# Gate scaling of expert rows on ScalarE, the conditioning row applied in the output stage, a fifth high-part buffer, and small VectorE operations issued earlier

## The chip, the cores and the metric

One core of a Trainium2 chip runs the whole program. The metric is the device time of one execution in microseconds (us). The core has TensorE (matmuls, PE in the profile; its weight loads are PEld), VectorE (DVE), ScalarE (ACT), GpSimd (POOL), SyncE (SP, which here only issues DMAs) and 16 DMA engines.

## The reference

One layer of a decoder trunk on 512 tokens of width 1024, all in float32: a mixing sub-layer (retention and dilated attention), then a mixture of experts, then a final RMSNorm. The change touches the end of it:

```
mod = silu(c) @ w_ada + b_ada -> sh_a, sc_a, gt_a, sh_f, sc_f, gt_f     # rows of 1024
x = x + gt_a * (merged @ w_o)                                          # "x1"
h = rms_norm(x, g_ffn) * (1 + sc_f) + sh_f
top 4 of 32 experts per token, gates = softmax(top logits)
expert e: u = h @ w1[e] + b1[e]            # 1024 -> 2048
          a = min(u_even, 7) * sigmoid(1.702 * min(u_even, 7)) * (clip(u_odd, -7, 7) + 1)
          y_e = a @ w2[e] + b2[e]          # 1024 -> 1024
x = x + gt_f * sum over chosen e of gate[token, e] * y_e
out = rms_norm(x, g_final)
```

The conditioning row `gt_f` has one value per column and is the same for all tokens; the gate has one value per token and expert.

## The kernel before, in words

A float32 product is made on TensorE from parts: the high part of a weight tile is a rounded copy (ScalarE, line 1039, `prep_hi`), the low part is the tile less its high part (VectorE, line 1045, `prep_lo`), and TensorE multiplies high by high, high by low and low by high.

The first 700 us or so are the conditioning rows, attention, retention and the merge. Weight tiles there go through a pool `wr` of five buffers. Around line 678 a tile `z` of that pool is filled with zeros and written to the spare rows of two arrays in HBM, `acc` (line 682) and `xn2` (line 683). Before the experts, the stream x1 is written to the first 512 rows of `acc` (line 903, `x1_store`).

Then the experts run one after the other, the first two in fixed order, the others sorted by their number of tokens. Each works on a block of gathered token rows: 96 slots for a large expert (`KIND` "L"), 64 for a small one ("S"). The order is four large ones, then large and small in turn. An expert has 12 weight tiles of 1 MB: eight of `w1` ("A", k = 0 to 7, 8 KB rows) and four of `w2` ("B", k = 0 to 3, 4 KB rows). The list `tiles` holds the order A of expert e, then B of expert e−1, then A of e+1, and so on. The order on every engine in this stage is the order of the program text (`manual_schedule`): the loop over `tiles` issues the matmuls of tile i, then `prep_hi(i + 3)`, `prep_lo(i + 3)`, then the small operations that belong to this place.

The tiles are loaded by SyncE into a ring of ten buffers (five of `wr`, one of `wb`, four of `hl`); `prep_lo(i)` issues the load of tile i + 10 behind it, since it is the last reader of its buffer. The high parts have four buffers (tag `mg`), the low parts four (tag `lo`); each comes free when TensorE has done its tile. For a large expert a tile takes 12 matmuls; for a small one the high and low parts of its 64 rows lie side by side as 128, a tile takes 8 matmuls, and the two halves are added at the end by a copy on ScalarE (`lower`) and matmuls with a shifted identity (`fold`).

Small operations around it: `evacuate` (at B k=0) reads `u` out of PSUM into `sg` (sigmoid, ScalarE, line 1197) and `av` (VectorE, lines 1202 and 1206). `times_gate` (VectorE, line 1209) finishes `av`; it stands behind A k=1 of the next expert, and for the last one at B k=2. TensorE transposes `av` before its tiles A k=3 and k=4 (line 1175, `turn`), and ScalarE and VectorE copy it out in two parts (lines 1116 and 1117). `slot_hot` (line 1140, at A k=5) prepares the gather of a later expert. `close` calls `finish`: VectorE makes `ys` = `y` × gate × `gtF` (line 1215; `gtF` is `gt_f` repeated over the partitions, loaded at line 1131), and GpSimd adds the rows of `ys` to `acc` in HBM by a scatter DMA with addition (line 1216).

After a loop for experts with more tokens than slots, which runs as often as a list says, the output stage loads `acc` in four blocks of 128 rows, by halves of 512 columns (line 1480), sums squares on ScalarE (line 1483), and VectorE multiplies by the root and by `g_final` (line 1491), and SyncE stores.

Of the kernel before, what the change touches and what calls it, by code (L numbers as in the profile page):

```python
# [11 lines left out]
F32 = mybir.dt.float32  # L12
F32R = mybir.dt.float32r
# [8 lines left out]
P = 128  # L22
# [14 lines left out]
NRA = 5  # L37
NRB = 1
NRC = 4
AHEAD = 3  # L40
TB = 1536
ROWS = S + P
# [71 lines left out]
def body(tc, a, out):  # L114
# [11 lines left out]
    def bcast(ap, off, n, parts=P):  # L126
        return dram(ap, off, [[0, parts], [1, n]])
# [9 lines left out]
    xn2 = nc.dram_tensor("s_h2", [ROWS, D], F32).ap()  # L137
    acc = nc.dram_tensor("s_acc", [ROWS, D], F32).ap()
    modr = nc.dram_tensor("s_mod", [1, 4096], F32).ap()
    btab = nc.dram_tensor("s_bias", [4, 896], F32).ap()  # L140
# [540 lines left out]
    G.memset(z, 0.0)  # L681
    G.dma_start(acc[S:], z)
    G.dma_start(xn2[S:], z)
# [105 lines left out]
    mx = ExitStack()  # L789
    wb = mx.enter_context(tc.tile_pool(name="wrB", bufs=NRB, side="right", reuse_waits="tile"))  # L790
    rt = mx.enter_context(tc.tile_pool(name="rt", bufs=1, side="right", reuse_waits="tile"))
# [90 lines left out]

    ring = [(wr, "wr")] * NRA + [(wb, "wb")] * NRB + [(hl, "hl")] * NRC
    rs = {}
# [7 lines left out]
    def half_row(t, n):  # L892
        return xs[:, t, n * 512:(n + 1) * 512]
# [8 lines left out]
    def x1_store(t, n):  # L902
        SP.dma_start(acc[t * P:(t + 1) * P, n * 512:(n + 1) * 512], half_row(t, n))

# [112 lines left out]
    sorted_i = rt.tile([1, E], I32, name="sorted_i")  # L1017
    for i in range(NRA + NRB):
        load(i, *ring[i])
# [14 lines left out]
    for k in range(NRC):  # L1034
        load(NRA + NRB + k, *ring[NRA + NRB + k])
    def prep_hi(i):
        if i < len(tiles) and i not in his:
            his[i] = mp.tile([P, 2048], F32R, name="w_hi", tag="mg")
            A.activation(his[i], loaded[i], AF.Copy)  # L1039
# [80 lines left out]
    for q in range(2):  # L1120
        turn_copy(xp0[q], slice(4 * q, 4 * q + 4), X[0])
    for i in range(1, AHEAD):
        prep_hi(i) if i not in his else None
        prep_lo(i)
    psx.close()
# [3 lines left out]
    A.activation(top7[:, 1:2], top7[:, 0:1], AF.Sigmoid, scale=1.702)  # L1129
    gtF = m1.tile([P, D], F32, name="gtF")  # L1130
    G.dma_start(gtF, bcast(modr, 3 * D, D))

# [79 lines left out]
    def finish(y, gate, idx):  # L1212
        n = idx.shape[0]
        ys = m2.tile([CAP, D], F32, name="ys", bufs=1)[:n]
        V.scalar_tensor_tensor(ys, y[:n].rearrange("p a b -> p (a b)"), gate, gtF[:n], op0=OP.mult, op1=OP.mult)  # L1215
        G.indirect_dma_start(out=acc, out_offset=bass.IndirectOffsetOnAxis(ap=idx[:, :1], axis=0), in_=ys,  # L1216
                             in_offset=None, compute_op=OP.add)
# [79 lines left out]
    hot_at = {(0, 0): 1, (0, 2): 0}  # L1297
    hot_at.update({(e, 5): e + 2 for e in range(E - 2)})
    sum_at = {(0, 1): 1, (0, 4): 0}
# [15 lines left out]
    for i, (kind, e, k) in enumerate(tiles):  # L1315
# [33 lines left out]
        else:  # L1349
# [26 lines left out]
            if e == 0 and k == 0:  # L1376
                ld = overflow_list()
        prep_hi(i + AHEAD)
        prep_lo(i + AHEAD)
        if kind == "A":  # L1380
            if nx is not None:
                SL[nx] = slot_rows(now["ps"], nx > 0)
            if e == 0 and k == 0:
                sort_counts()
            if (e, k) in hot_at:
                h_ = hot_at[e, k]
                now["oh"] = slot_hot((rk1 if h_ < 2 else rkp)[:, :, h_], slots_of(h_))
            if e and k == 1:
                AVS[e - 1] = times_gate(SG.pop(e - 1), AVS[e - 1])
            if e > 1 and k == 0:  # L1390
                close(e - 2)
            if e and k in (3, 4):
                if k == 3:
                    AT[e - 1] = at_tiles(e - 1)
                turn_copy(now["at", k - 3], slice(4 * (k - 3), 4 * (k - 3) + 4), AT[e - 1])
            if e + 1 < E and k in (5, 6):
                if k == 5:
                    X[e + 1] = x_tiles(e + 1)
                turn_copy(now["xt", k - 5], slice(4 * (k - 5), 4 * (k - 5) + 4), X[e + 1])
            if k == KC - 1:  # L1400
                if KIND[e] == "S":
                    now["low"] = lower(U[e])
                if e == 0:
                    evacuate(0)
            if e == 3 and k == 2:
                G.dma_start(lb.rearrange("p a b -> p (a b)"), bcast(ld, 0, 4 * E))
            if e == 5 and k == 2:
                V.tensor_copy(li, lb[0:1])
        else:
            if e + 1 < E:  # L1410
                if k == 0:
                    evacuate(e + 1)
                if e + 1 == E - 1 and k == 2:
                    AVS[e + 1] = times_gate(SG.pop(e + 1), AVS[e + 1])
                    AT[e + 1] = at_tiles(e + 1)
            if k == 3:
                if KIND[e] == "S":
                    now["ylow"] = lower(Y[e])
                if e >= E - 2:
                    close(e)  # L1420
# [3 lines left out]

    gfin = wr.tile([P, D], F32, name="gfin", tag="wr")
    SP.dma_start(gfin, bcast(a["g_final"], 0, D))
    extra = nc.values_load(li[0:1, 0, 2:3], min_val=0, max_val=E)  # L1427
    with tc.For_i(0, extra) as it:  # L1428
# [21 lines left out]
        for k in range(KC):  # L1450
            w = wb.tile([P, 2048], F32, name="w_x1", tag="wb")
            SP.dma_start(w, w1[0, ds(ev, 1)].rearrange("o (k p) n -> p (o k) n", p=P)[:, k])
            for j in range(4):
                PE.matmul(u[:, j], xT[:, k], w[:, j * 512:(j + 1) * 512], start=False, stop=(k == KC - 1))
# [9 lines left out]
        for k in range(4):  # L1464
            w = wb.tile([P, 2, D], F32, name="w_x2", tag="wb")
            SP.dma_start(w, w2[0, ds(ev, 1)].rearrange("o (k p) n -> p (o k) n", p=P)[:, 2 * k:2 * k + 2])
            for c in range(2):
                for n in range(2):
                    PE.matmul(y[:, n], aT[:, 2 * k + c], w[:, c, n * 512:(n + 1) * 512], start=False,
                              stop=(k == 3 and c == 1))  # L1470
# [3 lines left out]
    halves = [slice(n * 512, (n + 1) * 512) for n in range(2)]  # L1474
    at = [wr.tile([P, 2, D], F32, name="at", tag="wr") for _ in range(NT)]
    ss = [m2.tile([P, 2], F32, name="ss2", bufs=NT) for _ in range(NT)]
    with tc.manual_schedule():
        for t in range(NT):
            for c in halves:
                SP.dma_start(at[t][:, 0, c], acc[t * P:(t + 1) * P, c])  # L1480
        def scale_of(t):
            for n, c in enumerate(halves):
                A.activation(at[t][:, 1, c], at[t][:, 0, c], AF.Square, accum_out=ss[t][:, n:n + 1])  # L1483
            V.tensor_add(ss[t][:, 0:1], ss[t][:, 0:1], ss[t][:, 1:2])  # L1484
            return rms_cols(ss[t][:, 0:1], D, EPS, m2)
# [34 lines left out]
```

## Time and profile before

| | us |
|---|---|
| median of 3 runs (lowest, highest) | 1909.26 (1907.37, 1910.88) |
| profiled execution | 1909.79 |
| its span | 1908.0 |
| TensorE busy in the span | 1754.7 |
| VectorE busy | 1491.2 |
| ScalarE busy | 1052.6 |
| GpSimd busy | 463.7 |

The span runs from the first to the last instruction of the profiled execution; the execution's own time has 1.8 us around it. A busy TensorE is one that has a matmul in its pipeline. The granted clock is the share of TensorE's full speed (2.4 GHz) in a stretch. In a row of the waits, "A <- B" says that A's engine was idle until B was done. In a timeline a row ends with the idle time before it and what ended it.

### The profile page before, as it was taken

Reading aid. Unit: us, or ns where it says so; the run is one execution under the profiler, and the core shown is the slowest. Engines: PE = TensorE matmul, PEld = TensorE weight load, DVE = VectorE, ACT = ScalarE, POOL = GpSimd, SP = SyncE. Lnnn points to the kernel's source line nnn. Section 1 sums busy time; section 2 is a strip of 40 time slices with the busy share of each in tenths; the row PEclk is TensorE's granted clock in tenths of the full one; section 3 lists DMA queues with packets and bytes.
Section 4 is the critical chain, followed back from the end, with each engine's and each line's share of the span. In section 5 each row is a group of like instructions: output and inputs, shape, how many; then the busy total and the mean of one; then the engine's idle time right before and its main releaser. Section 6 shows DMA issues by size and latency. Waiting matters only on the chain. (4 is left out here: it accounts for less than half of the span.)

```text
span 1908.0 us, 23014 instructions
## 1 busy us (share of the span) xinstructions
PE 1754.7 (92%) x8369; PEld 1332.6 (70%) x8369; DVE 1491.2 (78%) x1506; ACT 1052.6 (55%) x968; POOL 463.7 (24%) x406
## 2 busy tenths in 40 slices
PE   5979999999999988999989989989889889889883
PEld 3868888888778865666666666666666667667662
DVE  7464535667653477999999999999999999999994
ACT  5133323222222334677677677677677677677672
POOL 2140001011110033253331231234462232232201
PEclk8999999999999989999999999999999999999997
DMA  9613333442673847999999999999999999999973
GB/s 313 167 45 97 103 90 117 123 117 84 180 184 111 297 149 269 326 382 361 367 381 348 369 380 355 373 378 358 372 373 371 368 381 361 368 379 359 373 298 103
DMA packets 206756, 521.27 MB, mean 273 GB/s; under 512 B 11974, under 2 KB 127094, under 8 KB 173744
## 3 DMA queue, kind: packets, MB, share of 16 engines
q1 hardware_dynamic: 197024, 492.36, 71.4%
q0 software_dynamic: 9616, 27.40, 6.1%
q8 instruction: 67, 1.10, 0.2%
q14 instruction: 49, 0.40, 0.1%
HBM read 501.57 MB, written 18.15 MB: 272 GB/s over the span
## 5 line engine op out<-in xcount | busy, mean ns | idle before, releaser
L1045 DVE TENSOR_TENSOR w_lo<-w_moe,w_hi 128x2048 fp32r<-128x2048 f32 x384 | 867.4, 2284 | 85.1 <-ACT w_hi L1039 84.5
L1039 ACT ACTIVATE w_hi<-w_moe 128x2048 fp32r<-128x2048 f32 x384 | 727.9, 1913 | 227.4 <-PE u L1339 164.3
L1339 PE MATMUL u<-w_hi,x 128*96 128x512 f32 x1152 | 315.8, 401 | 0.0
L1339 PEld LDWEIGHTS u<-w_hi,x 128*96 128x96 f32 x1152 | 180.3, 163 | 72.1 <-issue 0.2
L1216 POOL DMA_INDIRECT s_acc<-ys,idx x32 | 109.5, 3420 | 378.9 <-DVE ys L1215 368.5
L1155 POOL TENSOR_SCALAR sl<-sl,misc 96x1 f32<-96x1 f32 (+1 forms) x32 | 61.3, 1914 | 414.8 <-ACT sl L1154 414.8
L211 PE MATMUL pp<-hTh,w_hl 128*128 128x512 f32 x400 | 160.3, 401 | 0.0
L1339 PE MATMUL u<-w_lo,x 128*96 128x512 f32 x576 | 156.9, 394 | 0.0
L213 PE MATMUL pp<-hTh,w_hl 128*128 128x512 f32 x400 | 156.6, 391 | 0.0
L212 PE MATMUL pp<-hTl,w_hl 128*128 128x512 f32 x400 | 156.4, 391 | 0.0
L1364 PE MATMUL y<-w_hi,at 128*96 128x512 f32 x576 | 151.3, 396 | 0.0
L202 DVE TENSOR_TENSOR w_hl<-w_raw,w_hl 128x1024 fp32r<-128x1024 f32 (+1 forms) x66 | 87.8, 1343 | 76.4 <-ACT w_hl L201 76.4
L1344 PE MATMUL u<-w_hi,x 128*128 128x512 f32 x448 | 141.1, 440 | 0.0
L1344 PE MATMUL u<-w_lo,x 128*128 128x512 f32 x448 | 130.6, 417 | 0.0
L1364 PEld LDWEIGHTS y<-w_hi,at 128*96 128x96 f32 x576 | 91.7, 161 | 44.4 <-issue 5.9
L1339 PEld LDWEIGHTS u<-w_lo,x 128*96 128x96 f32 x576 | 93.5, 162 | 40.5
L1344 PEld LDWEIGHTS u<-w_lo,x 128*128 128x128 f32 x448 | 91.5, 204 | 22.5
L201 ACT ACTIVATE w_hl<-w_raw 128x1024 fp32r<-128x1024 f32 (+1 forms) x66 | 65.2, 1001 | 70.7 <-PE pp L213 54.0
L1175 PE MATMUL pt<-misc,av 96*128 96x96 f32 (+1 forms) x256 | 37.0, 274 | 70.9 <-DVE av L1209 70.9
L1344 PEld LDWEIGHTS u<-w_hi,x 128*128 128x128 f32 x448 | 85.8, 207 | 19.6 <-issue 5.4
L1175 PEld LDWEIGHTS pt<-misc,av 96*128 96x128 f32 (+1 forms) x256 | 28.6, 163 | 94.0 <-DVE av L1209 82.9
L211 PEld LDWEIGHTS pp<-hTh,w_hl 128*128 128x128 f32 x400 | 75.5, 189 | 18.0 <-issue 2.6
(344 smaller groups left out, 2922.9 us busy)
## 6 DMA issues: line engine op xcount, KB each, us to landing
w_moe<-in_w_mlp SPq DMA_DIRECT2D x384, 1024.0 KB, 7.9
w_raw<-in_w_in SPq DMA_DIRECT2D x76, 512.0 KB, 5.3
w_ada<-in_w_ada SPq DMA_DIRECT2D x24, 1024.0 KB, 5.4
w_raw<-in_w_ret_o SPq DMA_DIRECT2D x8, 512.0 KB, 4.3
w_o<-in_w_o SPq DMA_DIRECT2D x4, 1024.0 KB, 5.0
xin<-in_x SPq DMA_DIRECT2D x4, 512.0 KB, 6.6
w_raw<-in_w_att_o SPq DMA_DIRECT2D x8, 256.0 KB, 6.7
xs<-in_x SPq DMA_DIRECT2D x8, 256.0 KB, 5.9
```

Source lines behind the costliest of these rows:

```text
L201: A.activation(hi[:, :kc], raw, AF.Copy)
L202: eng.tensor_tensor(lo[:, :kc], raw, hi[:, :kc].bitcast(F32), op=OP.subtract)
L211: PE.matmul(ps, hi[:, k], mh[:, k], start=(k == 0), stop=False)
L212: PE.matmul(ps, hi[:, k], ml[:, k], start=False, stop=False)
L213: PE.matmul(ps, lo[:, k], mh[:, k], start=False, stop=(k == kc - 1))
L1039: A.activation(his[i], loaded[i], AF.Copy)
L1045: V.tensor_tensor(los[i], loaded[i], his[i].bitcast(F32), op=OP.subtract)
L1175: PE.transpose(pt[:, i, :n], rows[:, c * P:(c + 1) * P], ident[:n, :n])
L1216: G.indirect_dma_start(out=acc, out_offset=bass.IndirectOffsetOnAxis(ap=idx[:, :1], axis=0), in_=ys, in_offset=None, compute_op=OP.add)
L1339: PE.matmul(U[e][:CAP, j], s_[:, k], m_[:, j * 512:(j + 1) * 512], start=False, stop=(k == KC - 1 and s_ is xl))
L1344: PE.matmul(U[e][:, j], X[e][2][:, k], m_[:, j * 512:(j + 1) * 512], start=(k == 0 and m_ is hi), stop=False, skip_group_check=True)
L1364: PE.matmul(Y[e][:CAP, n], s_[:, 2 * k + c], m_[:, col:col + 512], start=False, stop=(k == 3 and s_ is al and c == 1))
```

## The change

The gate's product leaves VectorE: `ys` = `y` × gate is a ScalarE copy with a scale per row. `acc` now holds only the experts' sum, so all its rows are zeroed in the setup, and x1 goes to an array of its own, `x1d`. The output stage multiplies by `gtF` and adds x1 on VectorE, and the `gtF` tile of the expert stage is gone. The one buffer of `wb` leaves the ring of loads (nine are left) and becomes a fifth buffer for high parts; `prep_hi` is issued four tiles ahead instead of three. `times_gate` moves to B k=2 for all experts but the first, and `slot_hot` from A k=5 to A k=3. The overflow loop takes its weight buffers from the pool of low parts.

```diff
-NRB = 1
+NHB = 1
+AHEAD_HI = 3 + NHB
+    x1d = nc.dram_tensor("s_x1", [S, D], F32).ap()
...
-    G.dma_start(acc[S:], z)
+    for t in range(NT + 1):
+        G.dma_start(acc[t * P:(t + 1) * P], z)
...
-    ring = [(wr, "wr")] * NRA + [(wb, "wb")] * NRB + [(hl, "hl")] * NRC
+    ring = [(wr, "wr")] * NRA + [(hl, "hl")] * NRC
...
-        SP.dma_start(acc[t * P:(t + 1) * P, n * 512:(n + 1) * 512], half_row(t, n))
+        SP.dma_start(x1d[t * P:(t + 1) * P, n * 512:(n + 1) * 512], half_row(t, n))
...
     def prep_hi(i):
         if i < len(tiles) and i not in his:
-            his[i] = mp.tile([P, 2048], F32R, name="w_hi", tag="mg")
+            pool, tag = (mp, "mg") if i % (4 + NHB) < 4 else (wb, "wb")
+            his[i] = pool.tile([P, 2048], F32R, name="w_hi", tag=tag)
             A.activation(his[i], loaded[i], AF.Copy)
...
-    for i in range(1, AHEAD):
-        prep_hi(i) if i not in his else None
-        prep_lo(i)
+    for i in range(1, AHEAD_HI):
+        prep_hi(i)
+        if i < AHEAD:
+            prep_lo(i)
...
-    gtF = m1.tile([P, D], F32, name="gtF")
-    G.dma_start(gtF, bcast(modr, 3 * D, D))
...
-        V.scalar_tensor_tensor(ys, y[:n].rearrange("p a b -> p (a b)"), gate, gtF[:n], op0=OP.mult, op1=OP.mult)
+        A.activation(ys, y[:n].rearrange("p a b -> p (a b)"), AF.Copy, scale=gate)
...
-    hot_at.update({(e, 5): e + 2 for e in range(E - 2)})
+    hot_at.update({(e, 3 if e else 5): e + 2 for e in range(E - 2)})
...
-        prep_hi(i + AHEAD)
+        prep_hi(i + AHEAD_HI)
         prep_lo(i + AHEAD)
...
-            if e and k == 1:
-                AVS[e - 1] = times_gate(SG.pop(e - 1), AVS[e - 1])
+            if e == 1 and k == 1:
+                AVS[0] = times_gate(SG.pop(0), AVS[0])
...
-                if e + 1 == E - 1 and k == 2:
+                if k == 2:
                     AVS[e + 1] = times_gate(SG.pop(e + 1), AVS[e + 1])
-                    AT[e + 1] = at_tiles(e + 1)
+                    if e + 1 == E - 1:
+                        AT[e + 1] = at_tiles(e + 1)
...
-    gfin = wr.tile([P, D], F32, name="gfin", tag="wr")
+    rows2 = wr.tile([P, 2, D], F32, name="rows2", tag="wr")
+    gfin, gtF = rows2[:, 0], rows2[:, 1]
     SP.dma_start(gfin, bcast(a["g_final"], 0, D))
+    SP.dma_start(gtF, bcast(modr, 3 * D, D))
+    at = [wr.tile([P, 2, D], F32, name="at", tag="wr") for _ in range(NT)]
+    for t in range(NT):
+        SP.dma_start(at[t][:, 1], x1d[t * P:(t + 1) * P])
...
-    at = [wr.tile([P, 2, D], F32, name="at", tag="wr") for _ in range(NT)]
+    sqs = hl.tile([P, D], F32, name="sqs", tag="hl")
...
         def scale_of(t):
+            for c in halves:
+                V.tensor_mul(at[t][:, 0, c], at[t][:, 0, c], gtF[:, c])
+                V.tensor_add(at[t][:, 0, c], at[t][:, 0, c], at[t][:, 1, c])
             for n, c in enumerate(halves):
-                A.activation(at[t][:, 1, c], at[t][:, 0, c], AF.Square, accum_out=ss[t][:, n:n + 1])
+                A.activation(sqs[:, c], at[t][:, 0, c], AF.Square, accum_out=ss[t][:, n:n + 1])
```

## Rows read from the trace of the kernel before

**Rows 1.** The page, part 1: busy us, share of the span, instructions.
```profile
PE 1754.7 (92%) x8369; PEld 1332.6 (70%) x8369; DVE 1491.2 (78%) x1506; ACT 1052.6 (55%) x968; POOL 463.7 (24%) x406
```
**Rows 2.** Busy time by stretch: the turn of experts 5 to 30, and one pair.
```profile
core 0: us, PE busy (x) PEld busy (x) DVE busy (x) ACT busy (x) POOL busy (x), PEclk, DMA share, GB/s
894.50:1828.50 934.00, 870.32 (x3885) 618.17 (x3884) 870.20 (x547) 686.84 (x494) 288.42 (x203) 0.96 1.00 369
1398.60:1470.30 71.70, 66.72 (x300) 47.41 (x299) 66.95 (x44) 52.80 (x39) 35.06 (x18) 0.95 1.00 372
```
**Rows 3.** Waits of 850 to 1850 us: us in total, times, longest.
```profile
ACT w_hi L1039 <- PE u L1339: 128.7, 113, 1.8
...
PE pt L1175 <- DVE av L1209: 67.4, 14, 5.0
DVE w_lo L1045 <- ACT w_hi L1039: 66.7, 92, 1.6
```
**Rows 4.** Timeline of 1405 to 1417 us, VectorE, then TensorE: start, us, what.
```profile
1407.38 1.27 DVE L1215 SCALAR_TENSOR_TENSOR ys<-y,gate,gtF 64x1024 f32<-64x1024 f32 x1
1408.58 2.27 DVE L1045 TENSOR_TENSOR w_lo<-w_moe,w_hi 128x2048 fp32r<-128x2048 f32 x1
1410.77 1.27 DVE L1209 SCALAR_TENSOR_TENSOR av<-sg,top,av 96x1024 f32<-96x1024 f32 x1
...
1405.15 1.07 PE L1344 MATMUL u<-w_hi,x 128*128 128x512 f32 x4
1406.06 1.07 PE L1344 MATMUL u<-w_lo,x 128*128 128x512 f32 x4
1412.10 0.90 PE L1175 MATMUL pt<-misc,av 96*128 96x96 f32 x4 [4.98 <-DVE av L1209]
1412.71 2.06 PE L1344 MATMUL u<-w_hi,x 128*128 128x512 f32 x4
1414.56 1.82 PE L1344 MATMUL u<-w_lo,x 128*128 128x512 f32 x4
1416.22 0.49 PE L1175 MATMUL pt<-misc,av 96*128 96x96 f32 x4
```
**Rows 5.** Groups by line and shape, 850 to 1850 us: busy, mean ns, idle before.
```profile
L1197 ACT ACTIVATE sg<-u 96x1024 f32<-96x1024 f32 x15 | 15.0, 1003 | 0.0
...
L1187 ACT ACTIVATE low<-y 64x1024 fp32r<-64x1024 f32 x13 | 13.3, 1023 | 0.3
```
**Rows 6.** Instructions of the tile w_moe, 1398.6 to 1470.3 us: loads from issue to landing.
```profile
DMA to landing us min/median/max: 6.2/8.3/9.2
```
**Rows 7.** Busy time by stretch, of 35 and 20 us (columns as in rows 2).
```profile
1119.50:1154.50 35.00, 30.02 (x132) 21.55 (x132) 33.16 (x22) 23.58 (x18) 10.02 (x8) 0.90 1.01 387
1124.00:1144.00 20.00, 19.09 (x85) 14.19 (x86) 18.19 (x13) 14.44 (x13) 7.08 (x7) 0.86 1.01 405
```
**Rows 8.** Timeline of VectorE in the first expert.
```profile
724.19 2.29 DVE L1045 TENSOR_TENSOR w_lo<-w_moe,w_hi 128x2048 fp32r<-128x2048 f32 x1 [3.70 <-ACT w_hi L1039]
```
**Rows 9.** Waits of SyncE's queue, 300 to 420 us.
```profile
SPq L147 <- DMA s_h<-z: 11.1, 1, 11.1
```
**Rows 10.** Timeline of SyncE, ScalarE and VectorE, 320 to 370 us.
```profile
331.92 0.37 SPq L147 DMA_DIRECT2D w_ada<-in_w_ada  x1
332.40 21.63 SPq L190 DMA_DIRECT2D w_raw<-in_w_in  x6
...
349.77 2.18 ACT L227 ACTIVATE w_hl<-w_raw 128x512 fp32r<-128x512 f32 x4
...
364.92 0.61 DVE L263 TENSOR_SCALAR w_ada<-w_ada,cs 128x256 f32<-128x256 f32 x2
```
**Rows 11.** Timeline of the end, 1836 to 1908 us.
```profile
1870.34 1.27 DVE L1215 SCALAR_TENSOR_TENSOR ys<-y,gate,gtF 96x1024 f32<-96x1024 f32 x1
...
1884.40 1.28 DVE L1215 SCALAR_TENSOR_TENSOR ys<-y,gate,gtF 64x1024 f32<-64x1024 f32 x1 [9.94 <-ACTq L1428]
...
1894.22 0.63 ACT L1483 ACTIVATE at<-at 128x512 f32<-128x512 f32 x1 [10.74 <-DMA at<-s_acc]
1894.76 0.18 ACT L1483 ACTIVATION_READ_ACCUMULATOR at<-at 128x1 f32 x1
...
1901.94 2.74 DVE L1491 SCALAR_TENSOR_TENSOR at<-at,rms,gfin 128x512 f32<-128x512 f32 x4
```
**Rows 12.** Timeline of VectorE at 694 us: the residual's add.
```profile
694.48 0.69 DVE L900 TENSOR_TENSOR xs<-xs,o 128x512 f32<-128x512 f32 x1
```

More of the change, by code (lines that the diff above doesn't have):

```diff
@@ L789, in body @@
     mx = ExitStack()
-    wb = mx.enter_context(tc.tile_pool(name="wrB", bufs=NRB, side="right", reuse_waits="tile"))
+    wb = mx.enter_context(tc.tile_pool(name="wrB", bufs=NHB, side="right", reuse_waits="tile"))
     rt = mx.enter_context(tc.tile_pool(name="rt", bufs=1, side="right", reuse_waits="tile"))
@@ L1017, in body @@
     sorted_i = rt.tile([1, E], I32, name="sorted_i")
-    for i in range(NRA + NRB):
+    for i in range(NRA):
         load(i, *ring[i])
@@ L1034, in body @@
     for k in range(NRC):
-        load(NRA + NRB + k, *ring[NRA + NRB + k])
+        load(NRA + k, *ring[NRA + k])
     def prep_hi(i):
         if i < len(tiles) and i not in his:
-            his[i] = mp.tile([P, 2048], F32R, name="w_hi", tag="mg")
+            pool, tag = (mp, "mg") if i % (4 + NHB) < 4 else (wb, "wb")
+            his[i] = pool.tile([P, 2048], F32R, name="w_hi", tag=tag)
             A.activation(his[i], loaded[i], AF.Copy)
@@ L1450, in body @@
         for k in range(KC):
-            w = wb.tile([P, 2048], F32, name="w_x1", tag="wb")
+            w = wc.tile([P, 2048], F32, name="w_x1", tag="lo")
             SP.dma_start(w, w1[0, ds(ev, 1)].rearrange("o (k p) n -> p (o k) n", p=P)[:, k])
@@ L1464, in body @@
         for k in range(4):
-            w = wb.tile([P, 2, D], F32, name="w_x2", tag="wb")
+            w = wc.tile([P, 2, D], F32, name="w_x2", tag="lo")
             SP.dma_start(w, w2[0, ds(ev, 1)].rearrange("o (k p) n -> p (o k) n", p=P)[:, 2 * k:2 * k + 2])
```

## The prediction

> **What bounds the kernel now.** I read the page's busy shares first [rows 1]: TensorE at 92% and VectorE at 78% of the span say little, because the stages differ. So the second view is busy time by stretch. From 894.5 us (first low part of expert 5) to 1828.5 us (first low part of expert 31) the kernel repeats one pattern, a large expert and a small one in turn. One such pair takes 71.7 us; the stretch is 934.0/71.7 = 13.0 pairs, half of the run. In a pair VectorE is busy 66.95 us, TensorE 66.72 (at a granted clock of 0.95), ScalarE 52.80, and the DMA engines show a share of 1.00 at 372 GB/s [rows 2]. Three resources stand close together, so what ends the waits decides. The third view, the waits of 850 to 1850 us, has two that matter [rows 3]: TensorE waits for `av` at line 1209 (67.4 us in 14 waits, one per pair), and VectorE waits for the high part on ScalarE (66.7 us), which itself waited for TensorE to give a high-part buffer back (128.7 us). Nobody waits for a weight to land. The timeline of one such wait [rows 4] shows its mechanism: in the small expert, TensorE stops at 1407.1, because before tile k=3 it has to transpose `av` of the large expert, and VectorE still has `ys` (1.27), a low part (2.27) and `av` (1.27) to do. It resumes at 1412.1 after 4.98 us idle, and then at the lower of its two clocks (1.2 instead of 2.4 GHz): four matmuls take 1.85 and 1.66 us from start to start instead of 0.91. So the pair is bound by VectorE's order in the small expert and by the high-part buffers in the large one, in alternation, with the DMA close behind.
>
> **The change, part by part.** The floor of the pair for each engine:
> VectorE loses two `ys` (one per expert), each 1.20 us from its start to the next one's start (1407.38 to 1408.58) [rows 4]: 66.95 − 2.40 = 64.55 us.
> TensorE's own work: 71.7 less the 4.98 wait, less what the low clock costs behind it. That is 1.85 − 0.91 for one group of four, 1.66 − 0.91 for the next [rows 4], and some 0.4 for the transposes: 2.1. This leaves 64.6 us. The stall goes only if `av` is ready in time. Line 1209 moves from after tile A k=1 of the next expert to after B k=2, that is three tiles of low parts earlier (3 × 2.2 us), and `ys` ahead of it is gone as well (1.2): 7.8 us against a stall of 5.0. Behind it, three low parts come 1.2 us later each; they have a lead of up to three tiles. `slot_hot` moves two tiles earlier and costs nothing, since VectorE does the same work in sum.
> The fifth high-part buffer lets ScalarE convert one tile further ahead. When TensorE gives back a tile, the high part of the next low part is already there, so VectorE does not wait out the 1.9 us conversion. This is what makes up the 66.7 us [rows 3], and what is late next is TensorE itself (the low-part buffers stay four).
> ScalarE takes the two `ys`. The trace has no Copy of a 1024-column PSUM tile with a per-row scale. The nearest rows are 1.003 us (Sigmoid, 96 rows) and 1.023 (Copy, 64 rows) [rows 5]; I take 1.02, both ends within 0.1. 52.80 + 2.04 = 54.8 of 71.7: not a bound. For a small expert this copy waits for the fold matmuls behind tile A k=0, and the next high parts queue behind it; their extra buffer covers that (cost 0; 2.5 us per pair if the cover is gone).
> The ring of loads goes from ten buffers to nine. Landing takes 6.2 to 9.2 us in a pair [rows 6]; nine tiles at 2.9 us are 26 us from one use of a buffer to the next, eight of them before the high part is made: cost 0 as long as the DMA queue keeps up.
> The DMA is the third floor. A pair moves 71.7 us × 0.372 = 26.7 MB. How fast could it? The share of 1.00 allows two readings: full, or merely never empty. Bounds: 372 GB/s as now gives 71.7 us (no gain); the best 20 us, 405 GB/s, give 65.9. The best stretch as long as half a pair, so with gather, scatter-add and both kinds of weight rows in it, is 387 GB/s [rows 7]: 69.0 us. I take a little less, 68.5, since even in that stretch TensorE had its stall (30.02 busy of 35.00), so the queue was not fed as it will be. It is the highest of the three floors: gain 3.2 us per pair, 13.0 pairs, **−42 us**; bounds 0 and 7.1 × 13 = −92 (all engines at their floors).
>
> A rule speaks against this. The Trainium skill, page "DMA: Bandwidth & Descriptors", section Specifications, gives a limit of about 358 GB/s from HBM for one core; by it a pair would need 26.7/0.358 = 74.6 us, and nothing could be won. The trace already disagrees: 369 GB/s mean over 934 us [rows 2]. The same page (section on the iDMA fabric) reports a lone load stream at 408.7; by that figure the pair's estimate is 65.3 us.
>
> **Start of the expert stage.** High part 4 now comes before the copy at line 1256, which TensorE holds up; VectorE waited 3.70 us for that high part [rows 8]. Gain 0 to 3.7; I take 1, because TensorE is held by VectorE's sorting there.
>
> **Setup.** Four more zeroing DMAs of 512 KB from GpSimd, 0.5 us of issue each, in a stretch where GpSimd idles. The `z` tile holds a buffer of the weight pool; SyncE already waits 11.1 us for its last store before it issues `w_ada` and the next `w_raw` [rows 9]. Two stores need some 7 us, so four more hold it 2 to 8 us longer. The loads are issued from 331.9 on and first used at 349.77 (`w_raw`) and 364.92 (`w_ada`) [rows 10]; with 5 us to land, 11 us of cover: cost 0 (5 if it is gone).
>
> **End.** The last expert's `ys` goes to ScalarE (1.02 for 1.28, −0.3). Expert 30's `ys` at 1870.34 stands ahead of the copies TensorE waits for [rows 11]: −1.2. The output stage grows: per 128 rows two multiplies and two adds of 128x512 on VectorE, by the residual's add 0.69 us each [rows 12]: 16 × 0.69 = 11.0 us. Before, VectorE's last operation there ended at 1904.68, 10.5 us after the first half row landed (1894.22) [rows 11]. Now each of four row blocks takes VectorE 2.75 (the four) + about 0.9 (waiting in order for ScalarE's second Square, 0.63 + 0.19) + 0.3 + 1.4 = 5.35, together 21.4: **+11** (8 if the Square is covered, 13 with the last power on GpSimd). The loads of `x1d`, gate row and final row (2.6 MB on SyncE) go out while SyncE and the DMA idle after 1850: 0.
>
> **Sum.** Profiled execution 1909.8 (0.5 above the median of the runs): −42 − 1 − 1.5 + 11 = −33.5, so **1876 us**; the likeliest case's own range is 1860 to 1892.
>
> **Rivals.**
> A, DMA already full (slower side): 1.00 is a real limit, tiles are only eaten at the speed at which they come, and everything won upstream turns into waits for landings. Price: the end's +9.5 stands alone, 1909.8 + 9.5 − 1 = 1918. It decides from the point at which a pair gains less than 0.65 us (8.5/13). For it: the share, and GB/s that hardly vary in the stretch. Against: no engine waits for a weight, landing 8.3 us is far from the 26 us that a full queue of nine would show, and 405 GB/s over 20 us. The Trainium skill's limit (the page above) points this way.
> B, the stall only changes its name: TensorE no longer waits for `av`, but for low parts, since VectorE falls behind in the small expert anyway; only the 2.4 us of `ys` are saved per pair. −31 − 2.5 + 11 = 1887. For it: four low-part buffers as before. Against: VectorE's 4.8 us of waits per pair are also open to be won.
> C, no DMA limit: pairs at 65.9 (405 GB/s): −75 − 2.5 + 11 = 1843. For it: the floors 64.55 and 64.6. Against: two engines would both have to be over 97% busy.
> D, ScalarE becomes the bound in order: `ys` waits for the fold and delays high parts by 2.5 us in each pair, which eats most of the gain: 3.2 − 2.5 left × 13 = −9, 1909.8 − 9 + 8.5 = 1909. Against: 17 us of idle ScalarE per pair.
>
> **Numbers.** Forecast 0.42, A 0.18, B 0.20, C 0.14, D 0.06. A measurement of this kernel tells from no change what is over 0.2%, some 4 us. Faster: forecast, B, C, and a little of D, 0.77; same 0.05 (D, and the edge of A); slower 0.18 (A). The range 1846 to 1916 leaves out the lower half of C and the upper half of A, 0.16.
>
> **What would show it.** Right: the wait of TensorE on line 1209 gone from the waits, its granted clock 1.00 through the pair, VectorE's wait for the high part cut to a third, pairs of 67.5 to 69.5 us, GB/s near 387, landing well above 8.3 us; VectorE 21 us long in the output stage. Wrong: engines that wait for `w_moe` landings at 372 GB/s (A), TensorE that waits for line 1045 (B), GB/s above 400 (C), VectorE waiting for line 1039 behind the new `ys` (D); or an end that costs under 5 us.

## The result and the profile after

The changed kernel takes 1890.01 us (median of 4 runs, 1888.09 to 1891.61) against 1909.26: a ratio of 0.9896, 95% interval 0.9884 to 0.9908. It is faster by 19 us, inside the range of 1846 to 1916; the forecast was 1876. Here and below a ratio leaves out the runs that lie over 1.5% above the fastest of their kernel, so for two experiments whose times scatter (e1 and e4) it lies below the ratio of the medians. Its profiled execution took 1888.8 us with a span of 1887.0.

The page's busy line (before: [rows 1]), then busy time by stretch: the turn of experts 5 to 30, and two neighbouring pairs in it (columns as in [rows 2]).
```profile
PE 1747.2 (93%) x8369; PEld 1327.1 (70%) x8369; DVE 1465.3 (78%) x1490; ACT 1084.0 (57%) x1000; POOL 651.0 (34%) x409
```
```profile
889.90:1802.10 912.20, 862.70 (x3886) 612.23 (x3885) 837.69 (x522) 711.60 (x519) 496.39 (x201) 0.98 0.99 378
1385.90:1454.80 68.90, 65.09 (x299) 46.01 (x299) 64.47 (x42) 54.76 (x41) 44.99 (x16) 1.00 1.01 385
1454.80:1524.50 69.70, 66.36 (x299) 47.11 (x299) 64.44 (x42) 54.84 (x41) 26.03 (x16) 0.98 1.00 378
```
The stretch was 934.0 us [rows 2] and is 912.2. The pair's median over the 13 is 69.6 us (before 71.7), and one pair, the first, takes 77.8. The columns to look at are VectorE's 64.4 (it was 66.95) and, unlooked-for, GpSimd's: 288 us of the stretch before [rows 2], 496 now, on as many instructions (203 and 201). Stage by stage, the span's 21.0 us are: −4.6 up to expert 5, −21.8 in the stretch, −4.3 from there to the last low part, +9.7 behind it.

The waits of 850 to 1830 us (before: [rows 3]), each with the us in total, the number of waits and the longest:
```profile
PE pt L1178 <- DVE at L1121: 41.5, 17, 3.3
DVE av L1205 <- ACT sg L1200: 39.1, 28, 2.5
PE pt L1178 <- DMA xg<-s_h,idx: 7.0, 1, 7.0
DVE w_lo L1049 <- ACT w_hi L1043: 0.6, 2, 0.4
```
TensorE's wait for `av` (67.4 us) is gone, and so is VectorE's for the high part (66.7, now 0.6). A new wait stands at the same transpose line: TensorE waits for the copy `at` on VectorE. The timeline of one (VectorE, then TensorE), to be held against [rows 4]:
```profile
1391.49 11.09 DVE L1049 TENSOR_TENSOR w_lo<-w_moe,w_hi 128x2048 fp32r<-128x2048 f32 x5
1402.51 0.41 DVE L1143 TENSOR_TENSOR oh<-misc,rkp 128x256 bf16<-128x256 f32 x1
1402.84 0.55 DVE L1121 TENSOR_TENSOR at<-pt,at 128x384 fp32r<-128x384 f32 x1
...
1403.44 0.55 PE L1178 MATMUL pt<-misc,xg 96*128 96x96 f32 x4 [3.34 <-DVE at L1121]
```
The transposes of the next expert's rows (k=5) need a buffer of `pt` in PSUM, where TensorE's results lie, and there are two of them. One comes free when VectorE has read the low part of `at` out of it, and that instruction stands behind five low parts of 2.2 us. Right ahead of it stands `oh`, 0.33 us from its start to the copy's: this is `slot_hot`, which the change itself moved to this place. VectorE no longer pauses for high parts, and its order is what TensorE meets.

The 77.8 us pair, in the timeline of GpSimd, VectorE and TensorE:
```profile
899.41 21.88 POOL L1219 DMA_INDIRECT s_acc<-ys,idx  x1 [10.48 <-ACT ys L1218]
...
921.91 9.05 POOL L1161 TENSOR_TENSOR sl<-sl 64x1 f32<-64x1 f32 x1
931.02 8.74 POOL L1162 CAST idx<-sl 64x1 int32<-64x1 f32 x1
940.03 3.54 POOL L1166 DMA_INDIRECT xg<-s_h,idx  x1 [0.28 <-POOL idx L1162]
...
928.63 11.08 DVE L1049 TENSOR_TENSOR w_lo<-w_moe,w_hi 128x2048 fp32r<-128x2048 f32 x5
...
951.00 0.66 PE L1178 MATMUL pt<-misc,xg 64*128 64x64 f32 x4 [7.03 <-DMA xg<-s_h,idx]
```
GpSimd comes free at 921.29, behind a scatter whose issue took 21.88 us. A few operations of 64x1, a cast last, then compute the index `idx` of the rows that the gather fetches into `xg`. An addition usually takes 0.19 us and the cast 0.18; here they take 9.05 and 8.74, and the cast ends where VectorE's run of low parts ends (939.7). The gather goes out late, and TensorE stands 7.03 us. That is the clue which the experiments follow: GpSimd is held, that is, its instructions last many times their usual length, while VectorE is busy.

VectorE in the output stage, first and last row (before: [rows 11]): 1863.21 to 1883.92, 20.7 us.
```profile
1863.21 0.69 DVE L1492 TENSOR_TENSOR at<-at,rows 128x512 f32<-128x512 f32 x1 [19.48 <-DMA at<-s_acc]
...
1881.19 2.73 DVE L1503 SCALAR_TENSOR_TENSOR at<-at,rms,rows 128x512 f32<-128x512 f32 x4
```

### The profile page after: what moved, and what is told of

The parts are those of the page before. It is cut to its first block, busy times and chain, and to the rows that moved or that the text cites. A ratio compares the mean times of both kernels' runs of the same rounds, so it can differ in the third digit from the quotient of the medians.

```text
span 1887.0 us, 23253 instructions
## 1 busy us (share of the span) xinstructions
PE 1747.2 (93%) x8369; PEld 1327.1 (70%) x8369; DVE 1465.3 (78%) x1490; ACT 1084.0 (57%) x1000; POOL 651.0 (34%) x409
## 4 chain that ended last, share of the span: by engine, by line
PE 81%; DVE 9%; issue 5%; POOL 2%; DMA 2%; ACT 1%; SPq 0%; DVEq 0%; POOLq 0%; ACTq 0%
PE u L1342 21%; PE y L1367 10%; PE u L1347 8%; PE pp L213 6%; PE pp L215 6%; PE pp L214 6%; PE y L1374 5%; DVE w_lo L1049 3%; PE pp L247 2%; PE pp L245 2%; PE pp L246 2%; PE pt L1178 2%; PE u L1138 1%; POOL s_acc L1219 1%; PE y L740 1%
## 5 line engine op out<-in xcount | busy, mean ns | idle before, releaser
L1219 POOL DMA_INDIRECT s_acc<-ys,idx x32 | 258.9, 8090 | 251.2 <-ACT ys L1218 235.6
L1342 PEld LDWEIGHTS u<-w_hi,x 128*96 128x96 f32 x1152 | 181.5, 164 | 72.8 <-issue 0.6
L1158 POOL TENSOR_SCALAR sl<-sl,misc 96x1 f32<-96x1 f32 (+1 forms) x32 | 105.8, 3305 | 327.4 <-ACT sl L1157 327.4
L204 DVE TENSOR_TENSOR w_hl<-w_raw,w_hl 128x1024 fp32r<-128x1024 f32 (+1 forms) x66 | 91.3, 1397 | 72.3 <-ACT w_hl L203 72.3
L1347 PE MATMUL u<-w_hi,x 128*128 128x512 f32 x448 | 136.2, 427 | 0.0
L1347 PE MATMUL u<-w_lo,x 128*128 128x512 f32 x448 | 126.3, 405 | 0.6 <-DVE w_lo L1049 0.6
L203 ACT ACTIVATE w_hl<-w_raw 128x1024 fp32r<-128x1024 f32 (+1 forms) x66 | 65.2, 1002 | 70.7 <-PE pp L215 54.1
L278 POOL DMA_DIRECT2D s_mod<-brow x16 | 7.9, 492 | 281.1 <-DVE brow L275 228.4
L213 PEld LDWEIGHTS pp<-hTh,w_hl 128*128 128x128 f32 x400 | 75.5, 189 | 18.1 <-issue 2.6
L215 PEld LDWEIGHTS pp<-hTh,w_hl 128*128 128x128 f32 x400 | 75.4, 188 | 16.2
```

The source lines that it names most:

```text
L204: eng.tensor_tensor(lo[:, :kc], raw, hi[:, :kc].bitcast(F32), op=OP.subtract)
L213: PE.matmul(ps, hi[:, k], mh[:, k], start=(k == 0), stop=False)
L215: PE.matmul(ps, lo[:, k], mh[:, k], start=False, stop=(k == kc - 1))
L1158: G.tensor_scalar(sl[:, 6:7], sl[:, 2:3], misc[:n, 258:259], misc[:n, 257:258], op0=OP.mult, op1=OP.add)
L1342: PE.matmul(U[e][:CAP, j], s_[:, k], m_[:, j * 512:(j + 1) * 512], start=False, stop=(k == KC - 1 and s_ is xl))
L1347: PE.matmul(U[e][:, j], X[e][2][:, k], m_[:, j * 512:(j + 1) * 512], start=(k == 0 and m_ is hi), stop=False, skip_group_check=True)
```

## The experiments

Each time is a median beside runs of the kernel before on the same chip (medians 1908.5 to 1911.2); each ratio, with its 95% interval, is to these. "Late gather" means the row that names TensorE waiting for `xg`; waits are of 850 to 1830 us. The expectations of the first four runs state the theories with which I began; GpSimd is in none of them as the cause, and neither foresaw the losses of e1, e2 and e4 or how little e3 gains.

**The change in three parts.** Alone, on the kernel before: the fifth high-part buffer (ring of nine, `AHEAD_HI`); the two moves (`slot_hot`, line 1209 to B k=2); `ys` on ScalarE with the conditioning row in the output stage.
```
e1:  +AHEAD_HI = 3 + NHB ... +prep_hi(i + AHEAD_HI)          (all hunks of NRB/NHB)
e2:  +hot_at.update({(e, 3 if e else 5): e + 2 ...
     +if k == 2: AVS[e + 1] = times_gate(SG.pop(e + 1), AVS[e + 1])
e3:  +A.activation(ys, y[:n]..., AF.Copy, scale=gate)        (with s_x1, z, output stage)
```


> The kernel before with the fifth high-part buffer alone (nine load buffers, high parts four tiles ahead). Theory 1 (TensorE's waits for small VectorE operations that stand behind low parts set the pair of experts): VectorE's 4.8 us of waits for the high part per pair go, but TensorE's wait for av (4.98 us per pair) stays, so little is won: 0 to -13 us (0 to 1 us per pair). Theory 2 (the forecast's: the DMA is the highest floor, at about 387 GB/s): as much as the buffers allow, -20 to -40 us, with the GB/s rising towards 387.

> The kernel before with the two moves alone (the gate product of av at B k=2, slot_hot at A k=3). Theory 1: the wait for av is gone, and in its place TensorE waits before the transposes at A k=5 for the copy that frees their PSUM bank, since this copy now stands behind a run of low parts; 1 to 2 us per pair are left, -13 to -26 us. Theory 2: no wait of TensorE on VectorE is left, -35 us or more.

> The kernel before with ys on ScalarE, x1 in an array of its own and the longer output stage alone. The end costs 10 to 11 us in both theories. Theory 1: ys no longer stands ahead of av, the wait for av falls from 5.0 to about 3.8 us and VectorE has 2.4 us less per pair: -16 to -31 us in the experts, -6 to -20 in all. Theory 2: -25 us in all, as the work of VectorE is what goes.


Measured: e1 1990.56 us, ratio 1.0395 [1.0324, 1.0466]; e2 1962.61, 1.0287 [1.0269, 1.0304]; e3 1906.41, 0.9985 [0.9975, 0.9994]. Waits of e1, e2, e3:
```profile
PE pt L1178 <- DMA xg<-s_h,idx: 83.5, 8, 12.7
```
```profile
POOL idx L1159 <- DMA s_acc<-ys,idx: 65.2, 12, 6.9
PE pt L1175 <- DVE at L1117: 51.2, 13, 4.0
PE pt L1175 <- DMA xg<-s_h,idx: 32.1, 5, 7.4
```
```profile
PE pt L1175 <- DVE av L1209: 51.3, 14, 3.8
```
The parts alone are +81, +53 and −3 us; together −19.6. They are no terms of a sum. e3 has the waits for `av` of 3.8 us that Theory 1 gave it. In e2 the wait for `av` is gone and one for the copy has come, as Theory 1 had it, but of 3.9 us per pair in place of 1 to 2. The traced run of e1 took 2009.4 us, some 100 more than the kernel before, and late gathers make up 83.5 of them. Its timeline shows an addition of 64x1 on GpSimd that lasts 25 us and ends (1190.01) where VectorE's run ends, whose last row stands below it (1189.97):
```profile
1164.97 25.04 POOL L1159 TENSOR_TENSOR sl<-sl 64x1 f32<-64x1 f32 x1
...
1189.42 0.55 DVE L1143 TENSOR_TENSOR oh<-misc,rkp 128x384 bf16<-128x384 f32 x1
```
GpSimd instructions longer than 3.5 us between 880 and 1830 us, counted in the traces: 7 before, 47 after, 36 in e1, 37 in e2, 13 in e3.

**Copies first.** The changed kernel with the copies that free PSUM at A k=3 to 6 issued ahead of the high and low part of the same step.
```
+        if kind == "A":        # the turn_copy calls of k = 3, 4, 5, 6, moved up
         prep_hi(i + AHEAD_HI)
         prep_lo(i + AHEAD)
```


> The changed kernel with the four pairs of copies that free the transposes' PSUM banks (A k=3 to 6) issued ahead of the high and low part of the same step instead of behind them. Theory 1: TensorE's 3.3 us wait per pair for the copy goes, the pair falls from 69.5 to 66 to 67.5 us, 25 to 45 us less than the changed kernel (1845 to 1865 us), at 395 GB/s or more. Theory 2: the pair cannot fall under 68.5 us, so at most 13 us less (1877 us), and the landing times grow well above 8 us.


Measured: 1940.28 us, scattered from 1910 to 1963 (the traced run took 1952.9); ratio 1.0072 [1.0038, 1.0106]. Its waits, and one gather's issue on GpSimd:
```profile
PE pt L1178 <- DMA xg<-s_h,idx: 79.4, 11, 8.9
PE pt L1178 <- DVE at L1121: 16.5, 24, 0.8
```
```profile
1066.15 21.75 POOL L1166 DMA_INDIRECT xg<-s_h,idx  x1 [0.56 <-POOL idx L1162]
```
The wait for the copy falls from 41.5 to 16.5 us as meant, and the three pairs whose gather is in time take 66.7 to 68.1 us. But the other ten of thirteen take 75 to 78: the gather's issue, 0.99 us when free, is held 21.75. So a DMA issued by GpSimd is held as well.

From here on **Theory 3**: while VectorE runs instructions with two tensor operands back to back, GpSimd's small operations and DMA issues stand still, now and then getting in between two of them. The Trainium skill, page "SBUF — State Buffer", section "SBUF: two separate sides", names such a lock: a VectorE instruction with two SBUF inputs and a GpSimd one that reads SBUF exclude each other, each for one whole instruction. The traces agree that they exclude each other and disagree on the length: 9 to 25 us in the rows above, four and more low parts.

**VectorE stops for GpSimd.** One 0.15 us copy per expert on VectorE reads the gate that GpSimd computes behind the gather's issue, so VectorE stands until GpSimd is through. In the changed kernel, in the copies-first kernel, and in e1's.
```
         prep_hi(i + AHEAD_HI)
+        if kind == "B" and k == 0 and e + 3 < E:
+            V.tensor_copy(brk[:slots_of(e + 3)], SL[e + 3][1])
         prep_lo(i + AHEAD)
```


> The changed kernel with one instruction more per expert: a 0.1 us VectorE copy that reads the gate column which GpSimd computes behind the gather of the next expert's rows, so that VectorE stands still (some 2.5 us per expert, 5 per pair) until GpSimd has got through. Theory 3 (a run of back-to-back two-operand VectorE instructions locks GpSimd out; the fifth high-part buffer closed the gaps): no gather is issued later than some 6 us after its slot list, the stall of 8.3 us at 955 us goes, VectorE still has 69.5 - 64.5 - 5 = 0 us to spare per pair, so about 1880 to 1892. The rival (gathers are late because of the order of GpSimd's own queue, or of the DMA rings, and not because of VectorE): GpSimd's small operations stay as long as they were, and VectorE's wait is pure loss, 1 to 5 us per pair: 1900 to 1950.

> The same added copy in the changed kernel with its PSUM-freeing copies ahead of the conversions (the run that had pairs of 68.1 us where the gather was in time, and lost 85 us to late gathers). Theory 3: the 85 us of TensorE waiting for gathered rows fall below 10, the pairs take 68.1 to 70 us, 1865 to 1885, the fastest so far. The rival (GpSimd's or the rings' own order): no change of that wait, 1935 to 1960.

> The same added copy in the kernel before with the fifth high-part buffer alone (1990.6, 81 us slower than before, 83.5 us of it waits for gathered rows). Theory 3: nearly all of the 81 us go, 1900 to 1920, GpSimd's busy time falls from 836 to below 600. The rival: it stays above 1970.


Measured: e5 1941.83 us, 1.0171 [1.0135, 1.0207]; e6 1899.09, 0.9946 [0.993, 0.9963]; e7 1968.27, 1.0321 [1.0303, 1.0338]. Waits of e5, e6, e7:
```profile
DVE brk L1384 <- POOL gate L1171: 123.7, 27, 10.5
```
```profile
DVE brk L1393 <- POOL gate L1171: 89.0, 27, 10.0
PE pt L1179 <- DVE at L1121: 25.3, 26, 1.5
```
```profile
PE pt L1179 <- DVE av L1213: 86.7, 25, 5.5
DVE brk L1384 <- POOL gate L1171: 85.4, 26, 3.8
```
The times alone don't decide: e5's lies in the band of the rival, e6's between the two, and e7's at the edge of the rival's, 22 us below e1. The traces do: in all three no row of TensorE waiting for `xg` is left (e1 83.5 us, e4 79.4), of the 80 gather issues of 850 to 1830 us none took over 1.01 us, and GpSimd's busy time falls from 651 to 472 us in e5, from 693 to 514 in e6 and from 836 to 451 in e7. So late gathers come from VectorE's run, and GpSimd's own order as their cause falls. The times missed since the stop costs 3.3 to 4.6 us per expert at this place, ahead of a low part (e7 pays it in every pair, 75.1 us). The question is how to let GpSimd in cheaply.

**A break without a wait.** A VectorE memset of 128x1 behind each low part of the changed kernel.
```
         prep_lo(i + AHEAD)
+        V.memset(brk, 0.0)
```


> The changed kernel with a VectorE memset of 128x1 (no input, some 0.06 us) behind every low part, 24 per pair, about 1.5 us of VectorE time per pair and no wait. If the lock is held instruction by instruction and is let go as soon as one comes that has no second SBUF input, GpSimd gets in at every memset: its busy time falls from 651 to some 460, the stall at 955 us goes, 1880 to 1888. If the lock is held as long as VectorE has an instruction ready, whatever its form, nothing changes for GpSimd: busy 600 to 700 and 1887 to 1897.


Measured: 1900.59 us, 0.995 [0.9933, 0.9966], slower than without the memsets. Timeline of GpSimd, then VectorE:
```profile
1140.29 9.46 POOL L1160 TENSOR_TENSOR sl<-sl 64x1 f32<-64x1 f32 x1
1149.83 8.78 POOL L1162 TENSOR_TENSOR sl<-sl 64x1 f32<-64x1 f32 x1
...
1149.66 0.06 DVE L1384 MEMSET brk<- 128x1 f32 x1
...
1154.08 0.06 DVE L1384 MEMSET brk<- 128x1 f32 x1
...
1158.51 0.06 DVE L1384 MEMSET brk<- 128x1 f32 x1
```
Neither half of the expectation holds: GpSimd's busy time lies between the two (580 us) and the time above both. GpSimd does get in at a memset (its additions end just behind those at 1149.66 and 1158.51), but passes over others (1154.08): two pairs are still 9.4 us longer than the median for a late gather, with 14.9 us of TensorE's waiting in all. An instruction that needs no second operand is a chance and no sure way in.

**Less for GpSimd to do, and the stop at a better place.** ScalarE computes the row index (three instructions of 0.3 to 0.4 us) so that only the gather's issue is left for GpSimd, and VectorE's stop moves behind the low part, before `av`, where it waits for ScalarE anyway (39.1 us above). e9 in the changed kernel, e10 in the copies-first one.
```
-        G.tensor_scalar(sl[:, 6:7], ...), G.tensor_add x2, G.tensor_copy(idx, sl[:, 9:10])
+        A.activation(sl[:, 6:7], sl[:, 2:3], AF.Identity, scale=misc[:n, 258:259], bias=misc[:n, 257:258])
+        A.activation(sl[:, 7:8], sl[:, 0:1], AF.Identity, bias=sl[:, 1:2])
+        A.activation(idx, sl[:, 6:7], AF.Identity, bias=sl[:, 7:8])
...
+            V.tensor_copy(brk[:slots_of(e + 2)], SL[e + 2][3])   # in evacuate(e)
         AVS[e] = linear(u)
```


> The changed kernel with the row index computed by three ScalarE instructions in place of four GpSimd ones, so that GpSimd has only the gather's issue (0.99 us when it isn't held) to get through, and with VectorE's wait for GpSimd moved from before the low part to behind it, just before the instruction (av) at which VectorE waits some 1.4 us for ScalarE in any case. Theory 3: every gather is issued at that place and takes 0.99 us, VectorE's wait there costs at most 1 us more than before per expert (the run with the wait one low part earlier lost 4.6 per expert), the 8.3 us stall at 955 us goes, pairs stay at 69.5 to 70.5: 1878 to 1895. If what slowed the run with the wait was something else than its place (the wait of 4.6 us stays per expert), 1930 to 1945.

> The same two edits in the changed kernel with its PSUM-freeing copies ahead of the conversions (stall-free pairs of 68.1 us where gathers were in time; 70.4 with the wait ahead of the low part). Theory 3: no late gather and pairs of 68.1 to 69.5 us in all 13 pairs, so 912 us of the expert stretch become 886 to 905: 1861 to 1882, faster than both kernels. If the wait behind the low part costs as much as the one ahead of it, pairs stay at 70.4 and the time at 1890 to 1900.


Measured: e9 1896.4 us, 0.992 [0.9903, 0.9937]; e10 1890.18, 0.9882 [0.9866, 0.9899]. e10's median pair is 66.7 us, but its first takes 84.5 and another 83.0. Waits of e9, then of e10, and of e10 a gather's issue and the place of its second long pair in the timeline (GpSimd, ScalarE):
```profile
DVE brk L1311 <- POOL sl L1168: 38.6, 27, 10.6
ACT idx L1162 <- DMA s_acc<-ys,idx: 14.4, 1, 14.4
```
```profile
DVE brk L1311 <- POOL sl L1168: 58.5, 27, 10.2
ACT idx L1162 <- issue: 30.9, 5, 14.1
ACT idx L1162 <- DMA s_acc<-ys,idx: 14.1, 1, 14.1
```
```profile
1000.28 6.75 POOL L1166 DMA_INDIRECT xg<-s_h,idx  x1 [14.76 <-ACT idx L1162]
...
1666.04 23.82 POOL L1219 DMA_INDIRECT s_acc<-ys,idx  x1 [10.81 <-ACT ys L1218]
...
1696.15 0.29 ACT L1162 ACTIVATE idx<-sl 64x1 int32<-64x1 f32 x1 [14.15 <-issue]
```
Both times lie above what was expected of Theory 3. The stop's price is as meant: 1.1 us at 27 of its 28 places in e9. The gather's issue mostly does not take the 0.99 us expected: GpSimd comes to it ahead of the stop, and it is held until VectorE stops (here from 1000.28 to 1007.03, VectorE's low parts ending at 1006.22), which is early enough for TensorE. But `idx` has four buffers, and the one that ScalarE wants is still to be read by the scatter of four experts before, whose issue on GpSimd was held for 23.8 us. ScalarE stands 14 us, and with it everything behind it. The wait belongs to the index ring: at each of e10's six long stops ScalarE stands at this line. (e1, e2 and e5 show the same wait on GpSimd: `idx` for `s_acc`, 65.2 us in e2.)

**Eight index buffers.** e10 with `name="idx", bufs=8` for 4, nothing else.


> The run with the index on ScalarE and the copies first, with eight index buffers in place of four, and nothing else. In that run 20 of 26 experts took 33.2 or 33.4 us and six were late by 3.6 to 13 us; at each of the six ScalarE stood 3.8 to 14.1 us before it could write the index, whose buffer the held scatter of four experts before had not let go. Theory 3 with that as its last wait: the six fall to at most 3 us each, two at 930 and 1696 us still wait some 5 us for the scatter that lies ahead of the gather in GpSimd's queue; the expert stretch shrinks by 25 to 40 us, 1850 to 1866. The rival (ScalarE only showed a wait that GpSimd's queue makes in any case, since the gather stands behind the same scatter): the wait moves to VectorE's stop and the time stays at 1880 to 1894.


Measured: 1848.63 us (1847.96 to 1850.46), ratio 0.9684 [0.9671, 0.9697], a little below the 1850 to 1866 expected. It beats both kernels. The stretch of experts 5 to 30 and one pair, and its waits:
```profile
892.10:1764.00 871.90, 850.79 (x3886) 599.83 (x3885) 835.94 (x546) 732.32 (x594) 322.67 (x101) 1.00 1.02 393
1160.50:1227.20 66.70, 65.24 (x300) 46.03 (x299) 64.36 (x44) 56.32 (x47) 19.36 (x8) 1.00 1.02 394
```
```profile
DVE brk L1311 <- POOL sl L1168: 32.6, 27, 2.8
PE pt L1178 <- DVE at L1121: 16.1, 24, 1.4
ACT w_hi L1043 <- DMA w_moe<-in_w_mlp: 6.5, 12, 1.4
```
TensorE no longer waits for `xg`, nor ScalarE at the index. Scatters are still held (up to 23.8 us), and nobody waits for them. TensorE is busy 65.24 of 66.7 us and the loads run at 394 GB/s; which of the two sets the pace isn't shown. What eight index buffers would do in the changed kernel without the other edits wasn't tried; no wait for the index shows in its trace.

**The DMA by itself.** The changed kernel with the low part computed for 384 of 2048 columns and TensorE's passes over the weights' low part left out; every weight byte is still loaded.
```
-  for s_, m_ in ((xh, hi), (xh, lo), (xl, hi)):
+  for s_, m_ in ((xh, hi), (xl, hi)):            (likewise the other three loops)
```


> The changed kernel without the weights' low-part products: the low part is computed for 384 of 2048 columns only and TensorE's passes over it are left out, so VectorE, TensorE and ScalarE no longer set the pace and every weight byte is still moved. It measures what the weights' DMAs do by themselves. The prediction's floor (387 GB/s) says 68 to 70 us per pair, no faster than the changed kernel; if DMA was not the floor, pairs fall below 66 us (above 400 GB/s).


Measured: 1815.44 us (one run). Stretch and one pair, the weights' landing in that pair, and a wait:
```profile
858.40:1734.60 876.20, 663.90 (x2624) 440.51 (x2622) 313.11 (x522) 713.85 (x519) 101.68 (x201) 0.85 1.02 395
1128.00:1195.10 67.10, 51.87 (x202) 34.42 (x202) 24.10 (x42) 54.88 (x41) 8.01 (x16) 0.85 1.02 396
```
```profile
DMA to landing us min/median/max: 18.4/20.9/23.3
```
```profile
ACT w_hi L1043 <- DMA w_moe<-in_w_mlp: 141.7, 190, 2.4
```
Here the DMA is the bound: ScalarE waits 141.7 us for weights, a load lands 21 us after its issue, and with VectorE busy a third of its time a pair still takes 67.4 us (876.2/13), just below the 68 to 70 of the forecast's floor. It is no floor to the tenth: e12's stretch is shorter, 67.1 us per pair (871.9/13). GpSimd's busy time in the stretch is 101.68 us, against 496.39 with the low parts, and none of its instructions there takes over 1.5 us: with the stops of e5 to e7, this shows the hold to be VectorE's doing.

## Why the prediction was right in its range and wrong in its forecast

Of the 42 us forecast for the pairs 21.8 came, and the terms around them made up 7.7 us of what was missing. The range of 1846 to 1916 reaches over rival B, and B's time is nearly what was measured. So the range held by its width and in part by luck: the bound on which the forecast rested, the DMA, was never reached.

- **Up to expert 5**: −4.6 where −1 was forecast, and at another place. The low parts of expert 1 begin at 736.9 us against 737.0, so the first expert gains nothing; the gain falls in experts 1 to 4. No part alone has it (expert 5 begins at 898.6, 894.2 and 893.6 us in e1, e2 and e3, at 894.5 before and 889.9 here); its cause is open.
- **VectorE's floor, 64.55**: right (64.44 to 64.47).
- **The stall for `av` goes**: right. "what is late next is TensorE itself" is the sentence that failed. What came next was VectorE again: the copies behind a run of low parts (41.5 us in 17 waits). e4 shows it, 41.5 to 16.5 us by moving them, and e12 has 16.1. The prediction's claim that low parts "have a lead of up to three tiles" left out whatever else stands in that run, and `slot_hot`, taken to cost nothing, moved into it. TensorE's own work, worked out as 64.6 us, shows as 65.24 busy in e12's pair.
- **The DMA as the highest floor, 68.5 us**: wrong. e11, which the DMA bounds, takes 67.4 us at 395 GB/s, with landings of 21 us, and e12 67.1. The changed kernel, at 69.6 us and landings of 7.3 to 7.9, never came to it. A floor read from the best half pair of a kernel that was held elsewhere was too high by 1.1 or more. The mark that I had named ("landing well above 8.3 us") was the right one to look for, and it said no.
- **The gain per pair, 3.2 us**: measured 2.3 (934.0/13 = 71.8 to (912.2 − 77.8)/12 = 69.5), 13 times, less 8.3 once. That is nearly the size and the mechanism of rival B (the stall changes its name, 2.4 us per pair, 1887 us): TensorE waits behind low parts in the small expert. B's own sign, TensorE waiting for the low parts themselves (line 1045 before, 1049 now), is 0.6 us; it waits for a copy that stands behind them. In size B was the case that happened, with a chance of 0.20 where it should have led.
- **GpSimd** had a cost of 0 and no line in the prediction. It cost 8.3 us once here, and with a part of the change alone most of the 81 and 53 us (in e2's trace six pairs take 78.7 to 81.1 us, the other seven 72.3 to 72.8): the largest risk of this change was in no sum. The sign for it was in the profile before: there one `sl` addition took 2.27 us, the length of a low part, in 12 of 14 small experts, where its neighbour took 0.19, and another took 13.31; I read GpSimd's 24% as room. The two as groups of 850 to 1850 us (count, busy us, mean ns, idle before), and the longest one, from the timeline at the start of the pair of [rows 2]:
```profile
L1158 POOL TENSOR_TENSOR sl<-sl 64x1 f32<-64x1 f32 x14 | 27.6, 1970 | 1.1
...
L1156 POOL TENSOR_TENSOR sl<-sl 64x1 f32<-64x1 f32 x14 | 2.6, 186 | 0.0
```
```profile
1397.61 13.31 POOL L1165 TENSOR_TENSOR sl<-sl 96x1 f32<-96x1 f32 x1
```
- **ScalarE with both `ys`**: right, 54.8 us per pair, a `ys` of 1.10 where 1.02 was taken. Rival D falls with it: VectorE's wait for high parts is 0.6 us. **Ring of nine, `z`**: cost 0, right; SyncE waits for the zeroing stores twice, 5.6 us together, and that stays hidden.
- **End**: +9.7 behind the last low part, with VectorE 20.7 us long where 21.4 was worked out. Right (the loads of `x1d`, gate row and final row are 3.1 MB, not 2.6, and cost nothing). Ahead of it −4.3 where −1.5 was taken.
- **Rival A** (DMA already full at 372 GB/s) falls by e11 and e12: 393 to 395 GB/s were to be had. **Rival C** gave 65.9 us for a pair without a limit; the median of e12 is 66.7, and no repeating pair of any run was under 66.6.

## What to carry to other kernels

When three resources stand within a few per cent of each other in a stretch, ask what stands in front of each wait in the queue that will be full next; here it was a copy behind a run of low parts, for which TensorE waited only 0.7 us in all in the kernel before. An engine at 24% can still set the end if its few instructions are long because another runs: compare the mean of one small instruction with its shortest. And parts of a change whose sum is a gain can each be a loss: a ring that only has to outlast one late instruction (four index buffers or eight) decided between 1890 us in e10 and 1849 in e12.

## What the runs showed of the hardware

- An operation of 64x1 on GpSimd that takes 0.19 us took 25.04 us while VectorE ran without a pause, nearly all of it on instructions with two tensor operands (one of 96x1, 0.21 us alone, 30.88 in e1), and a gather's issue 21.75 in place of 0.99. The hold outlasts the boundaries between VectorE's instructions, also those where the instruction reads PSUM (the copies `at` in e1), and often a memset between them.
- A pause of VectorE lets GpSimd in. Of the GpSimd instructions over 3.5 us between 880 and 1830 us, 167 in the fourteen traces met a VectorE pause of over 0.1 us, and none of them lasted more than 1.4 us beyond the pause's start, about the length of a scatter's issue that isn't held (1.42).
- What decides whether GpSimd gets in at a boundary without a pause is open. It isn't the number of VectorE's long runs: between 880 and 1830 us, 26 runs before and 27 after lasted over 20 us without a pause over 0.2 us, with 7 and 47 held operations. Where the pauses fall against GpSimd's requests may differ; that wasn't tried by itself.
- The loads of one core went on at 395 GB/s over 876 us. The Trainium skill's figure of about 358 for one core (page "DMA: Bandwidth & Descriptors", Specifications), already exceeded in [rows 2], is not what bounds here.
